# Fewer input products per pair of heads and more for the last pair, in a two-layer hybrid backbone on one core

## The chip, the cores and the metric

The kernel runs on one core of a Trainium2 chip. The metric is the device time of one execution in microseconds; the median of several executions is compared.

## The reference

A trunk of 256 context tokens and 512 latent tokens, 1024 channels wide, passes through two layers. The last layer needs outputs for the 512 latent tokens alone.

```python
def token_mixer(hc, hl, cos, sin, w_in, rw, cv, at, w_branch, w_out, ctx_out):
    zc = hc @ w_in
    zl = hl @ w_in
    rwc, cvc, atc, gtc = jnp.split(zc, IN_SPLIT_POINTS, axis=-1)
    rwl, cvl, atl, gtl = jnp.split(zl, IN_SPLIT_POINTS, axis=-1)
    o_rw_c, o_rw_l = rwkv_branch(rwc, rwl, *rw, ctx_out)
    o_at_c, o_at_l = attention_branch(atc, atl, *at, cos, sin, ctx_out)
    o_cv_l = conv_branch(cvl, *cv)
    out_l = merge_branches(o_rw_l, o_cv_l, o_at_l, gtl, w_branch, w_out)
    ...
```

The input projection w_in feeds three branches: RWKV-7 time mixing (16 heads of 64, a delta rule scanned forward and backward), a convolution of width 31, and grouped-query attention with rotary positions. Each branch is projected, gated by a sigmoid of further columns of the input projection, and summed; an output projection and a squared-ReLU MLP follow.

## The kernel before

The mixer of each layer runs in two stages: `rwkv_phase`, in which the time mixing is computed for eight pairs of heads, one after the other, and `merge_phase`, which holds attention, the convolution's norm and the projections.

**Jobs and units.** The input projection is cut into jobs of 128 output columns (`in_job`, `job`). A job has eight k steps, called units here. `fill(n)` issues n units: each has three products (high weights by high input, high by low, low by high), over 768 tokens as two matmuls of 384 columns each in layer 0, and over 512 tokens as one matmul of 512 columns each in most jobs of layer 1 (k, v and the rows 8 to 11 below run over 768 there too). Every fourth unit takes a new half of the weights, which `weight_half` loads on SyncE's queue and splits with one ScalarE and one VectorE operation.

**Spills.** 36 of the jobs produce columns that are needed only later: 8 tiles of queries (rows 0 to 7), 4 of keys and values (rows 8 to 11) and 24 of gates (rows 12 to 35). `spill` computes one and stores it to the scratch tensor z in HBM, from which `merge_phase` loads it again. The list `todo` gives their order: rows 0 to 19, 28 to 35, 20 to 27.

**A pair.** Iteration p of the loop in `rwkv_phase` queues the jobs of pair p+1 (k, r, v, some spills, two of the convolution), fills the first eight or so units, and then weaves generators: for pair p the merge (`rw_merge`, L928), the batch (`rw_batch`) and the chain over 12 chunks (`rw_chain`, L987 to L1006), the readout of pair p-1 (`rw_readout`), and for pair p+1 the preparation (`prep`), which ends in the solve (`rw_solve`), a serial run of VectorE operations between two kinds of transposes (L886 at its start, L895 and L896 at its end). The next iteration's merge needs the solve's result. `rw_kk` begins the preparation with the squares of k (L721). Each `yield` of a generator names some microseconds, and `pe` turns them into units at the rate that `weave` is given: the queued units by `span` for pairs 0 to 6, the setting `last` for the last one. The iteration of the last pair queues no pair but all spills that are left, and adds `att_stats`.

**How many spills each iteration gets.** `early` spills go into the opening. `todo_c(p)` spreads 32 - `rest` of them over the iterations 0 to 6. The others wait for the last pair. With `rest` at 9 these are 3, 4, 3, 3, 3, 4, 3 in both layers, and then 9 in layer 0 and 8 in layer 1.

**The load stage of attention.** `att_prep` loads keys, values and queries from z, turns the keys (`rope`, L522) and transposes the values (L590), and issues what is left of the jobs in parts: a third of them behind each of the two keys, half of the rest behind each of the two values. `merge_phase` issues the last of them, closes the pool of the input's halves hh and hl, and opens in its place the pool of the operand's halves oh and ol for the first projection.

The text above is program order. When the kernel is built, a scheduler orders each engine's instructions by this order and by what its own model holds ready, so a unit may run ahead of an instruction that waits. `behind` ties the merge's first matmuls to stand after the last unit issued ahead of the weave.

Of the kernel before, what the change touches and what calls it, by code (L numbers as in the profile page):

```python
# [44 lines left out]

SCHED = [dict(open=1.3, early=4, tap0=1, tap2=0, step=1.0, merge=1.2, sums=0, rest=9, ln=9, pad=1, last=1.15, span=78),
         dict(open=1.2, early=5, tap0=0.8, tap2=0, step=1.0, merge=1.4, sums=0, rest=9, ln=9, pad=1, last=0.85, span=76)]


def shape_constants():
# [24 lines left out]
class Kern:  # L77
# [1088 lines left out]
    def rwkv_phase(s, l, P, T):  # L1166
# [3 lines left out]
        with ExitStack() as rc:  # L1170
# [22 lines left out]
            lat = T != TOK  # L1193
            F = s.sched = SCHED[l]
            s.tdebt, s.tratio = 0.0, F['tap0']
# [298 lines left out]
```

## Time and profile before

| | us |
|---|---|
| median of 3 runs | 4302.82 |
| lowest and highest run | 4300.85, 4306.18 |
| profiled execution | 4305.05 |
| its span, first to last instruction | 4303.3 |
| mean granted clock over the span | 0.969 |

The profile comes from one execution; the predicted changes are made against its time. TensorE is the busiest engine. A busy engine in the profile has an instruction under way; matmuls overlap, so the same busy time can hold few or many of them, and the count beside it tells which. The granted clock is given as a share of 2.4 GHz, and 0.50 is its lower level.

In layer 0 the merges of the eight pairs begin at 223.0, 355.5, 496.5, 632.5, 773.5, 913.0, 1054.5 and 1195.0 us, and in layer 1 at 2592.0, 2707.5, 2833.5, 2961.0, 3081.0, 3199.0, 3322.5 and 3440.5 us (to half a microsecond). The stretches in the rows below run from one to the next; the last pairs end at about 1310 and 3519.5 us, where the load stage begins.

### The profile page before, as it was taken

To read this page: it belongs to the slowest core of one execution; us is meant where nothing else is said; L and a number is where in the kernel's file an instruction comes from. 1 tells how busy PE (TensorE), PEld (TensorE's weight loads), DVE (VectorE), ACT (ScalarE), POOL (GpSimd) and SP (SyncE) were. 2 spreads that over 40 slices of the span, in tenths; PEclk is the share of its full clock that TensorE was granted. 3 is DMA by queue.
4 is the path that set the end of the run, shared out by engine and by line. 5 is a ranking of instruction groups with operands and counts; after the bars stand their busy time and mean duration, and the time that the engine had idled before them with its cause. 6 is when DMAs were issued, how large, how long until landed. Compare 5 with 4: busy or idle time off the path is not lost.

```text
span 4303.3 us, 76623 instructions
## 1 busy us (share of the span) xinstructions
PE 4083.1 (95%) x31232; PEld 3360.6 (78%) x31232; DVE 2712.4 (63%) x5126; ACT 1829.2 (43%) x3426; POOL 254.8 (6%) x221
## 2 busy tenths in 40 slices
PE   6999999999998989899999899999999989898998
PEld 4988888888886679689999677877777765575886
DVE  3788888898855554332233478788889855554344
ACT  3444444444434442332222355455555534433332
POOL 0000000000001022100000200000000000121001
PEclk8999999999999999999999899999999979998998
DMA  4212221112134234343332131112122232242332
GB/s 167 80 49 63 59 62 57 49 55 71 58 102 165 70 116 154 126 147 118 101 98 62 64 90 54 55 59 59 59 65 61 84 125 76 68 138 61 96 96 79
DMA packets 443591, 367.70 MB, mean 85 GB/s; under 512 B 19662, under 2 KB 391528, under 8 KB 437096
## 3 DMA queue, kind: packets, MB, share of 16 engines
q1 hardware_dynamic: 422504, 283.10, 21.9%
q10 hardware_dynamic: 20736, 79.70, 5.1%
q8 instruction: 247, 4.05, 0.4%
q14 instruction: 104, 0.85, 0.1%
HBM read 301.38 MB, written 53.48 MB: 82 GB/s over the span
## 4 chain that ended last, share of the span: by engine, by line
PE 78%; DVE 11%; ACT 4%; issue 3%; DMA 2%; POOL 2%; SPq 0%; ACTq 0%; DVEq 0%; POOLq 0%
PE mm L412 29%; PE mm L389 21%; PE g L828 3%; PE g L634 2%; PE g L955 2%; PE g L966 2%; PE sp L987 2%; PE sp L991 2%; PE S L613 1%; PE g L875 1%; PE g L1071 1%; PE yp L1006 1%; DVE wl L332 1%; DVE A L892 1%; DVE Z L891 1%
## 5 line engine op out<-in xcount | busy, mean ns | idle before, releaser
L328 ACT ACTIVATE wh<-raw 128x512 fp32r<-128x512 f32 x700 | 441.4, 631 | 1218.4 <-PE mm L389 562.9
L332 DVE TENSOR_TENSOR wl<-raw,wh 128x512 fp32r<-128x512 f32 x700 | 500.6, 717 | 692.8 <-ACT wh L328 678.6
L412 PE MATMUL mm<-hh,wh 128*128 128x384 f32 (+1 forms) x2072 | 658.9, 378 | 10.0 <-ACT hh L347 4.0
L412 PE MATMUL mm<-hl,wh 128*128 128x384 f32 (+1 forms) x2072 | 626.0, 362 | 7.2 <-POOL hl L330 7.2
L412 PE MATMUL mm<-hh,wl 128*128 128x384 f32 (+1 forms) x2072 | 619.1, 361 | 2.5 <-DVE wl L332 2.4
L472 DVE SCALAR_TENSOR_TENSOR cv<-u,dw,cv 128x783 f32<-128x783 f32 (+1 forms) x480 | 426.7, 889 | 1.5
L412 PEld LDWEIGHTS mm<-hh,wh 128*128 128x128 f32 x2072 | 367.8, 191 | 61.8 <-issue 9.8
L412 PEld LDWEIGHTS mm<-hl,wh 128*128 128x128 f32 x2072 | 383.9, 191 | 34.4 <-POOL hl L330 10.0
L412 PEld LDWEIGHTS mm<-hh,wl 128*128 128x128 f32 x2072 | 384.0, 192 | 29.8 <-DVE wl L332 4.5
L412 PE MATMUL mm<-oh,wh 128*128 128x384 f32 (+1 forms) x768 | 252.3, 383 | 10.4 <-DVE acc L1320 6.0
L412 PE MATMUL mm<-ol,wh 128*128 128x384 f32 (+1 forms) x768 | 240.0, 365 | 10.6 <-POOL ol L330 10.6
L389 PE MATMUL mm<-hh,wh 128*128 128x384 f32 (+1 forms) x768 | 239.1, 366 | 6.3 <-ACT hh L347 3.6
L389 PE MATMUL mm<-hl,wh 128*128 128x384 f32 (+1 forms) x768 | 238.2, 365 | 5.5 <-POOL hl L330 5.0
L412 PE MATMUL mm<-oh,wl 128*128 128x384 f32 (+1 forms) x768 | 239.4, 365 | 0.0
L389 PE MATMUL mm<-hh,wl 128*128 128x384 f32 (+1 forms) x768 | 235.8, 362 | 0.0
L389 PE MATMUL mm<-fh,wh 128*128 128x384 f32 (+1 forms) x768 | 230.0, 353 | 0.0
L389 PE MATMUL mm<-fh,wl 128*128 128x384 f32 (+1 forms) x768 | 229.9, 353 | 0.0
L389 PE MATMUL mm<-fl,wh 128*128 128x384 f32 (+1 forms) x768 | 229.5, 352 | 0.0
L412 PEld LDWEIGHTS mm<-oh,wh 128*128 128x128 f32 x768 | 139.9, 190 | 51.5 <-ACT wh L328 13.6
L993 ACT ACTIVATE S<-sp,lam 128x64 f32<-128x64 f32 x352 | 94.4, 310 | 192.1 <-PE sp L991 172.4
L389 PEld LDWEIGHTS mm<-hh,wh 128*128 128x128 f32 x768 | 142.2, 192 | 37.7 <-ACT wh L328 15.9
L892 DVE TENSOR_TENSOR A<-A,Z 128x30 f32<-128x30 f32 (+14 forms) x480 | 159.0, 331 | 12.2
(300 smaller groups left out, 7078.5 us busy)
## 6 DMA issues: line engine op xcount, KB each, us to landing
raw<-in_w_in_dram SPq DMA_DIRECT2D x316, 256.0 KB
raw<-in_w_ff_dram SPq DMA_DIRECT2D x256, 256.0 KB
wmod<-in_w_mod_dram ACTq DMA_DIRECT2D x48, 1024.0 KB
raw<-in_w_branch_dram SPq DMA_DIRECT2D x96, 256.0 KB
z<-f ACTq DMA_DIRECT2D x40, 384.0 KB
gt<-z SPq DMA_DIRECT2D x24, 384.0 KB
raw<-in_w_out_dram SPq DMA_DIRECT2D x32, 256.0 KB
z<-f ACTq DMA_DIRECT2D x32, 256.0 KB
```

The costliest lines, as they stand in the source:

```text
L328: s.last_hi = nc.scalar.activation(out=hi, in_=src, func=AF.Copy)
L332: nc.vector.tensor_tensor(out=lo, in0=src, in1=hi.bitcast(F32), op=ALU.subtract)
L389: nc.tensor.matmul(ps[:, b, :t1 - t0], lhsT=w[:, k % 4, :], rhs=a[:, t0:t1], start=k == 0 and f == 0, stop=k == KT - 1 and f == 2)
L412: s.last_mm = nc.tensor.matmul(s.jps[:, b, :t1 - t0], lhsT=w[:, k % 4, :], rhs=a[:, t0:t1], start=k == 0 and f == 0, stop=k == KT - 1 and ...
L472: s.tap_pin(nc.vector.scalar_tensor_tensor(out=hold['c'], in0=u[:, k:k + L], scalar=w(k), in1=hold['c'], op0=ALU.mult, op1=ALU.add))
L634: nc.tensor.matmul(op[:, :nq], lhsT=V[:, kk, kv * 128:kv * 128 + 128], rhs=PT[:, kk, :nq], start=kk == 0, stop=kk == nk // 128 - 1)
L828: nc.tensor.matmul(gp[h][:, q, 0:n, :], lhsT=BK[ROWS[h], 4 * g + q].rearrange("p a b -> p (a b)"), rhs=E[ROWS[h], 0:n, 4 * g + q, :], star ...
L892: nc.vector.tensor_tensor(out=X[:, k + 1:, 0:k], in0=X[:, k + 1:, 0:k], in1=tm, op=ALU.add)
L955: nc.tensor.matmul(wu[ROWS[h], q - q0], lhsT=TT[ROWS[h], q, :], rhs=KM[ROWS[h], q].rearrange("p a b -> p (a b)"), start=True, stop=True)
L966: nc.tensor.matmul(ap[ROWS[h], q - q0, 0:n, :], lhsT=W[ROWS[h], q, :], rhs=GB[ROWS[h], h, q, 0:n, :], start=True, stop=True)
L987: nc.tensor.matmul(sp[ROWS[h], d], lhsT=GB[d][:, h, q[d], 0, :], rhs=UV[d][:, h * 12 + q[d], :], start=d == 0, stop=d == 1 and k == 0)
L993: nc.scalar.activation(out=Sn[:, d], in_=sp[:, d], func=AF.Copy, scale=Q['lam', d][:, q[d]:q[d] + 1])
```

## The change

Three settings of the table `SCHED` change: `rest` from 9 to 11 in layer 0, and in layer 1 `rest` from 9 to 14 and `last` from 0.85 to 1.4.

```diff
-SCHED = [dict(open=1.3, early=4, tap0=1, tap2=0, step=1.0, merge=1.2, sums=0, rest=9, ln=9, pad=1, last=1.15, span=78),
-         dict(open=1.2, early=5, tap0=0.8, tap2=0, step=1.0, merge=1.4, sums=0, rest=9, ln=9, pad=1, last=0.85, span=76)]
+SCHED = [dict(open=1.3, early=4, tap0=1, tap2=0, step=1.0, merge=1.2, sums=0, rest=11, ln=9, pad=1, last=1.15, span=78),
+         dict(open=1.2, early=5, tap0=0.8, tap2=0, step=1.0, merge=1.4, sums=0, rest=14, ln=9, pad=1, last=1.4, span=76)]
```

The places that read them:

```python
            todo_c = lambda p: round((32 - F['rest']) * p / 7)
...
                    spills(todo_c(p + 1) - todo_c(p))
...
                else:
                    spills(len(todo))
...
                s.weave(len(s.jobs) / F['span'] if more else F['last'], *gs)
```

## Rows read from the trace of the kernel before

**Rows 1.** The page's first part: busy time, share of the span, instructions.
```profile
PE 4083.1 (95%) x31232; PEld 3360.6 (78%) x31232; DVE 2712.4 (63%) x5126; ACT 1829.2 (43%) x3426; POOL 254.8 (6%) x221
```

**Rows 2.** Layer 0, iterations 1, 2, 3, 6, last pair, load stage; busy by engine, clock.
```profile
core 0: us, PE busy (x) PEld busy (x) DVE busy (x) ACT busy (x) POOL busy (x), PEclk, DMA share, GB/s
355.50:496.50 141.00, 140.42 (x1469) 122.45 (x1469) 121.72 (x231) 68.98 (x138) 1.80 (x4) 1.00 0.21 62
496.50:632.50 136.00, 135.53 (x1423) 115.85 (x1422) 116.97 (x225) 66.83 (x135) 1.66 (x4) 1.00 0.20 60
632.50:773.50 141.00, 139.79 (x1423) 120.35 (x1421) 119.19 (x229) 67.28 (x136) 1.26 (x4) 0.96 0.18 56
...
1054.50:1195.00 140.50, 139.67 (x1446) 119.90 (x1444) 122.34 (x232) 68.27 (x137) 1.66 (x4) 1.00 0.20 61
1195.00:1310.00 115.00, 113.57 (x1230) 101.12 (x1231) 56.66 (x115) 44.82 (x98) 0.00 (x0) 1.00 0.34 106
1310.00:1360.00 50.00, 36.17 (x144) 23.59 (x143) 30.27 (x50) 23.07 (x45) 13.62 (x8) 0.90 0.68 238
```

**Rows 3.** Starts of iterations 2 and 3: squares of k, then TensorE's clock in iteration 3.
```profile
501.32 0.94 ACT L721 ACTIVATE A<-E,V 128x768 f32<-128x768 f32 x1 [0.24 <-DVE E L656]
638.82 0.94 ACT L721 ACTIVATE A<-E,V 128x768 f32<-128x768 f32 x1 [1.85 <-DVE E L656]
...
644.00:648.00 4.00, 4.00 (x69) 0.50 0.22 66
```

**Rows 4.** Around layer 1's last merge: solve's ends, a spill's copy, the merge (timeline).
```profile
3403.74 1.99 DVE L886 STREAM_TRANSPOSE A<-Z 128x1024 f32<-128x1024 f32 x1
...
3422.78 0.58 ACT L1112 ACTIVATE f<-mm 128x512 f32<-128x512 f32 x1
...
3438.69 1.96 DVE L895 STREAM_TRANSPOSE Z<-A 128x1024 f32<-128x1024 f32 x1
...
3440.79 0.95 PE L928 MATMUL g<-Z,GL 32*32 32x32 f32 x48 [1.60 <-DVE Z L895]
```

**Rows 5.** Fill matmuls (tile mm) in layer 1's iterations 4, 5, 6 before the solve.
```profile
3081.00:3162.00 81.00, 28.16 (x91) 0.96 0.19 60
...
3199.00:3283.00 84.00, 37.85 (x122) 0.96 0.21 65
...
3322.50:3403.00 80.50, 30.84 (x107) 1.00 0.21 63
```

**Rows 6.** Layer 1, iterations 1, 2, 3, 5, 6, last pair, load stage, ten cold microseconds.
```profile
2707.50:2833.50 126.00, 124.34 (x1290) 103.71 (x1290) 99.54 (x207) 63.82 (x129) 1.02 (x4) 0.95 0.21 61
2833.50:2961.00 127.50, 125.52 (x1291) 100.88 (x1291) 113.41 (x234) 68.61 (x138) 1.58 (x4) 1.00 0.21 61
2961.00:3081.00 120.00, 115.14 (x1219) 90.92 (x1219) 102.98 (x218) 64.13 (x131) 1.15 (x4) 0.99 0.20 59
...
3199.00:3322.50 123.50, 121.82 (x1246) 96.28 (x1246) 106.38 (x223) 65.27 (x134) 1.08 (x4) 0.97 0.20 61
3322.50:3440.50 118.00, 114.66 (x1200) 87.39 (x1200) 99.02 (x211) 64.41 (x134) 0.99 (x4) 1.00 0.25 77
3440.50:3519.50 79.00, 77.25 (x849) 63.20 (x850) 39.03 (x100) 28.90 (x73) 0.00 (x0) 0.74 0.24 73
3519.50:3572.00 52.50, 38.96 (x139) 22.67 (x139) 29.12 (x47) 22.34 (x44) 12.24 (x9) 0.93 0.58 192
...
3480.00:3490.00 10.00, 10.00 (x71) 9.15 (x72) 1.59 (x12) 1.03 (x4) 0.00 (x0) 0.50 0.01 2
```

**Rows 7.** First rope matmul of each load stage, with TensorE's idle time before it.
```profile
1318.99 2.04 PE L522 MATMUL g<-kraw,rope 128*128 128x512 f32 x2 [5.64 <-DMA qs<-z]
...
3530.12 1.19 PE L522 MATMUL g<-kraw,rope 128*128 128x512 f32 x1 [6.88 <-DVE kT L582]
```

**Rows 8.** Dense runs of matmuls, of 384 columns and of 512 (chain in time).
```profile
1661.90 8.54 PE mm L412 x48
...
3375.24 6.05 PE mm L412 x25
```

## The prediction

> **What bounds the kernel now.** I read the page's first part, then busy time and granted clock by stretches of one pair of heads, then the order of instructions around the ends of pairs, then the load stage of attention. TensorE is busy 95% of the span [rows 1], but busy counts matmuls in flight, so what a removed job is worth must be read from the stage it leaves. The change moves jobs (one weight tile through eight k steps) between three places; each has its own limit.
>
> First, a pair of layer 0. Iterations 1 and 5 carry four spill jobs, the others three. The four-job iteration took 141.0 us; the three-job one behind it 136.0; a three-job one behind a three-job one 141.0 again [rows 2]. (Not shown: iterations 4 and 5 took 139.5 and 141.5.) So a job of 8.54 us of dense matmuls [rows 8] costs 5 us or nothing. The reason is seen at the starts [rows 3]: behind the four-job pair the squares of k (L721) waited 0.24 us for VectorE, behind the three-job pair 1.85 us; in the second case VectorE was still in the solve's last transposes when the merge began, TensorE ran dry, and the clock stood at 0.50, its lower level, 1.2 of 2.4 GHz. With less fill the solve on VectorE ends last, not the matmuls.
>
> Second, a pair of layer 1. It has two parts. The solve on VectorE runs from 3403.74 to the transpose at 3438.69 [rows 4], some 37 us, and TensorE fills it with whatever jobs are free. The part before it took 81.0 us with 91 recorded fill matmuls, 80.5 with 107 and 84.0 with 122 [rows 5]: above about 107 a job costs, below it time is flat, and the clock is 0.96 at 91 against 1.00 at 107. Thinning further buys little.
>
> Third, the last pair of layer 1. Its merge waited 1.60 us for the solve, and spill jobs of the last pair ended before it, the one at 3422.78 among them [rows 4]; I count five of eight there (3417 to 3440). Program order does not hold the jobs: whatever is free is put into the wait. So only three jobs were left for what follows, and the last pair ran at a mean clock of 0.74, with a stretch of 10.00 us busy out of 10 at 0.50 [rows 6], where layer 0's last pair, full of jobs, held 1.00 [rows 2].
>
> Behind both last pairs lies the load stage: the first rope matmul waits 5.64 us in layer 0 and 6.88 us in layer 1 for its tiles [rows 7], with the mean clock at 0.90 and 0.93 [rows 2, 6].
>
> **The change part by part.** No instruction is added or removed; only places change. From todo_c, spill jobs per iteration go in layer 0 from 3,4,3,3,3,4,3 and 9 to 3 each and 11; in layer 1 from 3,4,3,3,3,4,3 and 8 to 3,2,3,2,3,2,3 and 13. The last weave has 57.1 us of yields in layer 0, thus 65 units (a unit is one k step) before and after; what is left for the load stage goes from 7 to 23. In layer 1 it has 55.5: 47 units at 0.85, 77 at 1.4, and 17 and 27 left. A unit is 8.54/8 = 1.07 us in layer 0 and 3 x 6.05/25 = 0.73 us in layer 1 [rows 8].
>
> (a) Pairs of layer 0. Iteration 1 becomes a three-job pair behind an undisturbed one: 141.0 to 136.0, -5. Iteration 2 now stands behind a three-job pair and gets the late squares and the cold start: 136.0 to 140, +4. Iterations 3 and 4: 0. Iteration 5: 141.5 to 140, -1.5. Iteration 6, 140.5 now [rows 2], also loses its undisturbed start: +4. Sum +1.5. If no start were cold, all would be 136 and the sum -19; if the starts cost 5 and nothing is saved, +10. I take the middle rows, since both kinds of start stand in this trace.
>
> (b) Load stage of layer 0: 16 units more, 17.1 us. The wait of 5.64 us takes a first part; the 50 us at 0.90 give back up to 5.0 us if the work there is dense. 17.1 - 5.6 - 5.0 = +6.5. Bounds: 17.1 if all of it stands behind the waits, about 0 if it also fills the small waits for POOL's halves of the operand. Queued behind the extra units is the release of hh and hl, and so the operand splits; these also wait for loads of their own, issued behind the z loads, so I take no extra delay; the upper bound has room for it. The weight loads of the moved jobs (two per job, on SP's queue) may now stand ahead of the z loads, and their stores stay on ACT's queue; issues alone don't bound either queue, so I put them at nothing, and their cost, if that is wrong, is a longer wait for the rope [rows 7].
>
> (c) Pairs of layer 1, from the lengths of the iterations [rows 6]. Iteration 1 loses two jobs (those of k and v, which run over all 768 tokens): 126.0 to an ordinary 118.5, -7.5. Iteration 2 takes over these two and drops two of 512: 127.5 to a four-job length, 123.5, -4. Iteration 3 loses one: -1. Iteration 5 goes from four to two: 123.5 to 118.5, -5. Iterations 4 and 6: 0. Against this I set +3 for thinner pairs at a lower clock, since the clock already falls at 91 fill matmuls [rows 5]. Sum -14.5. Bounds: 0, if the lost clock eats it; -28, if all 29.0 us (5 jobs) came back as they do from 122 to 107 fill matmuls (3.6 us of matmuls, 3.5 us of time).
>
> (d) Last pair and load stage of layer 1: 40 units, +29.0 us of dense work. The last pair's 79.0 us at 0.74 lose 20.5 us to the clock; with 37 units instead of 7 behind the merge it is as full as layer 0's, and I take all of it back. The 10 extra units left over last 7.3 us and fit the 6.88 us wait. The 52.5 us at 0.93 give 3.7. 29.0 - 20.5 - 6.9 - 3.7 = -2.1. Bounds: +22 (no clock back) and -6.
>
> Sum: +1.5 + 6.5 - 14.5 - 2.1 = -8.6 us. The profiled execution took 4305.05 us, its span 4303.3; 4305.05 - 8.6 = 4296.5. The median of the runs shown is 2.2 us lower, so the forecast is 4302.8 - 8.6 = 4294.2 us.
>
> A rule to weigh at (d): the lower clock stands beside a TensorE that is busy throughout [rows 6], so here many small matmuls, without idle time, go with it. The Trainium skill (TensorE: Matmul & The Clock Gate, Part 1: The HAM clock gate) ties the lower level to TensorE standing idle and the upper to its being busy. By that rule alone the last pair would not be cold for want of fill, and fill would not warm it; its result is the third rival.
>
> **The rivals.** *Pairs follow TensorE's work.* If the step from 141.0 to 136.0 for one job (8.54 us) holds everywhere, each us removed gives 0.6: layer 0 -10, layer 1 -17.4, with (b) and (d) as above: -23, 4280 us. For it: TensorE's 95%. Against it: the flat 81.0 and 80.5 [rows 5].
>
> *Thinned pairs go cold.* Iterations 3 to 6 of layer 1 each lose about 3 us more to the clock, as the cold start [rows 3] costs 4 to 5: (c) is -2.5 and the sum +3.4, 4306 us. For it: the clock at 91 fill matmuls. Against it: 107 to 91 cost only 0.5 us.
>
> *The clock does not come back.* The last pair of layer 1 stays at 0.74 with more fill, so 29.0 us are paid with only the wait of 6.88 us as cover: (d) is +22, the sum +15.6, 4318 us, slower. It decides by degrees: below two thirds of the 24.2 us the gain is gone, and below 0.3 the kernel is slower by more than 8.6 us. Against it: 1.00 in layer 0's last pair [rows 2].
>
> *The load stage does not cover.* The built order may put the rope matmuls before the extra units; TensorE then waits as now with the units behind: (b) 17.1, (d) +8.5, sum +12.6, 4315 us, slower. Against it: in both layers the fill now stands ahead of that wait.
>
> That the jobs do not land where the settings say is true already (five of eight ran ahead of the merge) and only shifts part of (c) into (d); it stays inside the range.
>
> **How the numbers follow.** Forecast 0.58, TensorE's work 0.15, cold pairs 0.12, no clock 0.08, no cover 0.07. A measurement of this kernel can tell about 0.2%, 8.6 us, from no change; the forecast lies on that line, so half of its chance goes to each side. Faster: 0.29 + 0.15 = 0.44. Same: 0.29 + 0.12 = 0.41. Slower: 0.15. Eight times in ten: from 4280, where the first rival ends, to 4309, which takes in the cold pairs and leaves out the two slower ones; the bounds of (a) to (d) do not all fall together.
>
> **What the profile after would show.** (a) iterations 1 to 6 of layer 0 all near 140 us, cold starts at 2 and 6 too. (b), (d) the wait before the first rope matmul gone or below 2 us, and the load stage of layer 0 longer by 4 to 9 us. (c) iterations 1 and 5 of layer 1 near 118.5, iteration 2 near 123.5. (d) the last pair of layer 1 near 80 us with a clock above 0.95. What would make it wrong: a built order that differs in many places, so that pairs that I take over unchanged move too, or a clock that falls in the thinned pairs of layer 1 below 0.93.

## Result and profile after

The changed kernel took 4359.6 us (median of 4 runs, 4356.56 to 4365.12) beside 4304.5 us for the kernel before (median of 4 runs, the three of the first table and one more): ratio 1.0129, interval 1.0112 to 1.0147. It is 55 us slower; 4294.2 us was forecast, with a range that ended at 4309. Its profiled span is 4363.3 us at a mean clock of 0.961 (before 4303.3 and 0.969).

The page's first part shows the same instructions and more time on TensorE [rows 1]: the work did not grow, it took longer.

```profile
PE 4130.5 (95%) x31232; PEld 3397.3 (78%) x31232; DVE 2708.2 (62%) x5126; ACT 1831.3 (42%) x3426; POOL 253.5 (6%) x221
```

Busy time and clock by stretches say where: in layer 0 iterations 1 to 3 and the load stage, then in layer 1 iterations 1 to 6, the last pair, the load stage, and 20 us of the last pair (busy by engine with counts, clock, DMA share, GB/s).

```profile
354.00:489.50 135.50, 135.25 (x1422) 115.65 (x1421) 117.16 (x225) 66.84 (x135) 1.65 (x4) 1.00 0.20 60
489.50:630.50 141.00, 139.78 (x1423) 120.59 (x1421) 119.14 (x228) 67.33 (x136) 1.25 (x4) 0.96 0.18 56
630.50:771.50 141.00, 139.74 (x1421) 120.10 (x1420) 119.56 (x229) 66.83 (x136) 1.74 (x4) 0.96 0.18 54
1300.00:1360.00 60.00, 52.87 (x262) 44.39 (x260) 32.16 (x53) 27.33 (x50) 15.27 (x8) 0.94 0.68 235
2711.00:2840.00 129.00, 126.33 (x1295) 105.18 (x1295) 109.00 (x226) 65.43 (x131) 1.28 (x4) 0.96 0.18 54
2840.00:2967.00 127.00, 123.79 (x1263) 99.41 (x1263) 101.49 (x216) 65.71 (x133) 1.02 (x4) 0.97 0.21 61
2967.00:3095.50 128.50, 117.12 (x1193) 91.15 (x1193) 108.42 (x227) 62.42 (x128) 0.63 (x4) 0.94 0.17 49
3095.50:3221.00 125.50, 118.15 (x1211) 92.21 (x1211) 95.22 (x204) 63.96 (x130) 0.64 (x4) 0.96 0.18 55
3221.00:3355.50 134.50, 121.94 (x1192) 95.19 (x1192) 108.93 (x228) 62.36 (x128) 1.26 (x4) 0.89 0.16 46
3355.50:3489.00 133.50, 125.53 (x1207) 95.47 (x1207) 98.46 (x209) 65.01 (x133) 0.64 (x4) 0.92 0.23 68
3489.00:3574.00 85.00, 84.19 (x875) 69.00 (x875) 31.67 (x90) 31.01 (x75) 0.00 (x0) 0.74 0.26 79
3574.00:3630.00 56.00, 48.76 (x189) 32.17 (x190) 30.18 (x46) 24.22 (x48) 11.48 (x8) 0.97 0.67 213
3530.00:3550.00 20.00, 20.00 (x111) 17.11 (x112) 3.38 (x19) 2.78 (x8) 0.00 (x0) 0.50 0.10 27
```

Against [rows 6], iterations 3, 5 and 6 of layer 1 are longer by 8.5, 11.0 and 15.5 us, with fewer matmuls in two of them and 7 more in the last. TensorE's idle time grew in them: 12.6 us in iteration 5, where before had 1.7. So something other than TensorE ends last there. It is the solve. VectorE's timeline of iteration 5 of after: start, four operations in the middle, end.

```profile
3311.23 1.97 DVE L886 STREAM_TRANSPOSE A<-Z 128x1024 f32<-128x1024 f32 x1 [1.39 <-ACT Z L863]
...
3322.97 0.74 DVE L472 SCALAR_TENSOR_TENSOR cv<-u,dw,cv 128x512 f32<-128x512 f32 x1
3323.63 0.40 DVE L891 TENSOR_TENSOR Z<-A 128x234 f32<-128x234 f32 x1
3323.94 0.74 DVE L472 SCALAR_TENSOR_TENSOR cv<-u,dw,cv 128x512 f32<-128x512 f32 x1
3324.61 0.40 DVE L892 TENSOR_TENSOR A<-A,Z 128x234 f32<-128x234 f32 x1
...
3353.61 1.99 DVE L895 STREAM_TRANSPOSE Z<-A 128x1024 f32<-128x1024 f32 x1
```

L891 and L892 are the solve's serial steps. Between two of them stands a tap of the convolution (L472), one of the 31 products that it sums up for each tile: 0.66 us from its start to the next step's. From L886 to L895 this solve took 42.4 us; that of iteration 6 took 43.9, where before has 3403.74 to 3438.69, 35.0 us [rows 4]. The taps in the solves of iterations 5 and 6 of after, and in that of iteration 6 of before (VectorE's busy time on line 472 and its count, clock, DMA share, GB/s):

```profile
3311.00:3353.40 42.40, 14.08 (x19) 0.95 0.19 54
3443.40:3489.00 45.60, 14.19 (x19) 1.00 0.37 107
```

```profile
3403.70:3440.60 36.90, 5.26 (x7) 1.00 0.37 110
```

TensorE's timeline shows who waits: TensorE sat idle for 2.50 us before the last merge (1.60 before [rows 4]). The rope matmuls of the two load stages, by contrast, lost their waits [rows 7].

```profile
3489.46 1.49 PE L928 MATMUL g<-Z,GL 32*32 32x32 f32 x48 [2.50 <-DVE Z L895]
...
1312.85 1.96 PE L522 MATMUL g<-kraw,rope 128*128 128x512 f32 x4 [1.57 <-DMA rope<-in_rope_dram]
...
3588.28 1.96 PE L522 MATMUL g<-kraw,rope 128*128 128x512 f32 x4 [0.84 <-DMA qs<-z]
```

### The profile page after: what moved, and what is told of

Read it like the earlier page. It is cut to its first block, busy times and chain, and to the rows that moved or that the text cites. A ratio compares the mean times of both kernels' runs of the same rounds, so it can differ in the third digit from the quotient of the medians.

```text
span 4363.3 us, 76605 instructions
## 1 busy us (share of the span) xinstructions
PE 4130.5 (95%) x31232; PEld 3397.3 (78%) x31232; DVE 2708.2 (62%) x5126; ACT 1831.3 (42%) x3426; POOL 253.5 (6%) x221
## 5 line engine op out<-in xcount | busy, mean ns | idle before, releaser
L332 DVE TENSOR_TENSOR wl<-raw,wh 128x512 fp32r<-128x512 f32 x700 | 501.4, 717 | 700.4 <-ACT wh L328 686.8
L412 PE MATMUL mm<-hh,wl 128*128 128x384 f32 (+1 forms) x2072 | 634.8, 367 | 15.6 <-DVE wl L332 15.5
L412 PEld LDWEIGHTS mm<-hh,wh 128*128 128x128 f32 x2072 | 373.4, 194 | 66.8 <-issue 9.0
L472 DVE SCALAR_TENSOR_TENSOR cv<-u,dw,cv 128x783 f32<-128x783 f32 (+1 forms) x480 | 424.7, 885 | 0.9
L389 PE MATMUL mm<-hh,wl 128*128 128x384 f32 (+1 forms) x768 | 234.5, 360 | 0.0
L828 PEld LDWEIGHTS g<-E,BK 64*128 64x128 f32 x1536 | 141.1, 197 | 40.7 <-issue 22.6
L828 PE MATMUL g<-E,BK 64*128 64x128 f32 (+1 forms) x1536 | 163.3, 294 | 8.3 <-ACT key L912 2.7
```

What stands on the lines that cost most here:

```text
L332: nc.vector.tensor_tensor(out=lo, in0=src, in1=hi.bitcast(F32), op=ALU.subtract)
L389: nc.tensor.matmul(ps[:, b, :t1 - t0], lhsT=w[:, k % 4, :], rhs=a[:, t0:t1], start=k == 0 and f == 0, stop=k == KT - 1 and f == 2)
L412: s.last_mm = nc.tensor.matmul(s.jps[:, b, :t1 - t0], lhsT=w[:, k % 4, :], rhs=a[:, t0:t1], start=k == 0 and f == 0, stop=k == KT - 1 and ...
L472: s.tap_pin(nc.vector.scalar_tensor_tensor(out=hold['c'], in0=u[:, k:k + L], scalar=w(k), in1=hold['c'], op0=ALU.mult, op1=ALU.add))
L828: nc.tensor.matmul(gp[h][:, q, 0:n, :], lhsT=BK[ROWS[h], 4 * g + q].rearrange("p a b -> p (a b)"), rhs=E[ROWS[h], 0:n, 4 * g + q, :], star ...
```

## Experiments

Two theories. A: with fewer spill jobs per pair, the jobs of the next pair come earlier and reach into the wait for the solve. A tap is kept behind the VectorE operation ahead of it in program order (`tap_pin`), often one of those jobs; so it comes to stand between the solve's steps, and the pair ends later. B: the thinned fill itself is to blame, because TensorE goes cold (its clock falls to the lower level) or idle.

The table holds all kernels: layer 0's pairs 0 to 6; from layer 0's last merge to layer 1's first; layer 1's pairs 0 to 6; in these the sum of the seven solves (L886 to L895) and the taps in them; from layer 1's last merge to the end. All in us, from one profiled execution each (merge starts to half a microsecond). One execution can lie well off its kernel's median: that of e1_l0 by 14.4 us, those of e3_last, e7_bhold_last and e14_rest7 by about 7. Three kernels, before, e1_l0 and e15_l0_rest7, hold the same instructions in layer 1, in the same order on VectorE and ScalarE, and their pairs differ by up to 5 us, their ends by 5.5; smaller differences between two rows say nothing.

| kernel | ratio, interval | L0 pairs | between | L1 pairs | solves | taps | end |
|---|---|---|---|---|---|---|---|
| before | | 972 | 1397 | 848.5 | 241.9 | 41 | 862.8 |
| after | 1.0129, 1.0112 to 1.0147 | 965.5 | 1408.5 | 894 | 275.6 | 84 | 874.3 |
| e1_l0 | 1.0023, 1.0010 to 1.0036 | 968.5 | 1407.5 | 853.5 | 242.1 | 41 | 864.0 |
| e2_rest | 1.0145, 1.0122 to 1.0169 | 964.5 | 1392 | 892 | 266.9 | 72 | 882.2 |
| e3_last | 1.0035, 1.0020 to 1.0050 | 976.5 | 1395.5 | 858 | 253.0 | 53 | 865.6 |
| e4_hold | 1.0031, 1.0018 to 1.0044 | 961 | 1397 | 863.5 | 218.7 | 0 | 872.1 |
| e5_bhold | 0.9991, 0.9975 to 1.0007 | 964.5 | 1389 | 857.5 | 216.4 | 0 | 858.0 |
| e7_bhold_last | 1.0000, 0.9988 to 1.0012 | 967 | 1387 | 859 | 216.4 | 0 | 869.3 |
| e10_rest12 | 1.0052, 1.0033 to 1.0071 | 964 | 1398 | 858.5 | 254.6 | 59 | 876.4 |
| e11_rest_hold | 1.0042, 1.0028 to 1.0057 | 971.5 | 1387 | 859.5 | 217.9 | 0 | 882.3 |
| e12_hold_tap06 | 1.0015, 1.0001 to 1.0029 | 973.5 | 1386.5 | 866 | 214.8 | 1 | 862.0 |
| e13_rest7_hold | 1.0011, 1.0000 to 1.0021 | 976.5 | 1389.5 | 862 | 220.0 | 0 | 860.2 |
| e14_rest7 | 1.0013, 1.0004 to 1.0021 | 964.5 | 1396 | 848 | 238.5 | 27 | 866.9 |
| e15_l0_rest7 | 1.0036, 1.0022 to 1.0050 | 974.5 | 1406 | 852 | 242.1 | 41 | 858.5 |

**One part alone.** The three settings apart: e1_l0 has only layer 0's, e2_rest only layer 1's `rest`, e3_last only layer 1's `last`.

```diff
 e1_l0:   layer 0  rest=9   ->  rest=11
 e2_rest: layer 1  rest=9   ->  rest=14
 e3_last: layer 1  last=0.85 -> last=1.4
```

> Only the layer 0 half of the change: rest is 11 there, layer 1 stays as before. By the two traces layer 0 gives +3 us (its pairs 6 to 8 us shorter, its load stage 11 longer). Both theories say the same here: 3 to 6 us slower than before, 4308 to 4311 us, within what can be told from no change. If it takes more than 15 us, the loss is not in layer 1 and both theories fall.

> Only rest = 14 in layer 1; last stays at 0.85 and layer 0 as before. Theory A, taps in the solve: in iterations 1 to 5 as many convolution taps stand between the solve's transposes as in the changed kernel (12, 6, 18, 6, 19 in the built order, against 0, 8, 9, 4, 9 before), in iteration 6 only 7 instead of 19. Iterations 1 to 5 take about 30 us longer than before, iteration 6 about 7 (its part ahead of the solve), in all some 35 to 45 us slower than before: 4340 to 4350. Theory B, thinned pairs go cold and the fill is missing: the same 45 us over iterations 1 to 6, iteration 6 not shorter than in the changed kernel (133 us), and more on top from a last pair that is thinner still: 4355 or more.

> Only last = 1.4 in layer 1; both rest settings stay at 9, so no pair loses a job. Theory A: 19 instead of 7 taps stand in the solve of iteration 6, which gets about 8 us longer (126 instead of 118); the last pair gains at most that back: 3 to 10 us slower than before. Theory B: no pair is thinned, the last pair is denser and warmer: 0 to 8 us faster than before, iteration 6 at 118.

Layer 1's `rest` alone gives as large a loss as the whole change (the three parts don't add up): its pairs take 892 us, after's 894. In time all three missed theory A's figures, upwards: e1_l0 is some 10 us slower where both theories had 3 to 6, e3_last some 15 for 3 to 10, and e2_rest took 4354.8 us, above A's 4350 and at the edge of B's 4355. But iteration 6 of e2_rest took 125 us, as A had it, not B's 133; what A left out is the end, 19 us longer than before. e3_last is the cleanest single case: no job changes its pair, yet iteration 6 is longer, 128.5 us for 118 [rows 6], at a clock of 1.00 in both, so not by a cold TensorE. VectorE's timeline and TensorE's merge behind it:

```profile
3405.53 2.00 DVE L886 STREAM_TRANSPOSE A<-Z 128x1024 f32<-128x1024 f32 x1
...
3451.34 1.92 DVE L895 STREAM_TRANSPOSE Z<-A 128x1024 f32<-128x1024 f32 x1
...
3453.41 0.95 PE L928 MATMUL g<-Z,GL 32*32 32x32 f32 x48 [3.38 <-DVE Z L895]
```

The solve starts 80.8 us after the merge, as before (81.0), and then takes 45.8 instead of 35.0 us, with 19 taps in it for 7. Twelve taps, three weight splits and some 2 us more of waits in the chain make the 10.8 us.

**The taps held.** In layer 1 every tap is queued on VectorE behind the end of the solve that stands ahead of it in program order; nothing else in the program is changed. e4_hold does it to after, e5_bhold to before, e7_bhold_last to before with `last` at 1.4, e11_rest_hold to before with `rest` at 14.

```diff
     def tap_pin(s, ins):
         s.tc.keep_in_program_order(ins)
+        if s.solved is not None and s.sched is SCHED[1]:
+            s.behind(ins, s.solved)
...
-        nc.vector.transpose(out=s.Z[:, 768:1792].rearrange("p (u t) -> p t u", t=32), in_=X)
+        s.solved = nc.vector.transpose(out=s.Z[:, 768:1792].rearrange("p (u t) -> p t u", t=32), in_=X)
...
             s.tdebt, s.tratio = 0.0, F['tap0']
+            s.solved = None
```

> The changed kernel with one thing undone: in layer 1 every convolution tap is queued on VectorE behind the end of the solve that stands before it in program order, so none stands inside a solve (80 did). No other instruction is added or left out. Theory A: the solves of iterations 1 to 6 fall from 37 to 44 us to 29 to 34; the taps are then paid beside other work: 30 to 50 us faster than the changed kernel, 4310 to 4330. Theory B: the solves are not what lost the time; the part ahead of the solve stays at 85 to 90 us or grows by the taps that now stand there: 4345 or more.

> The kernel before with the taps of layer 1 queued behind the solve, as in e4_hold, and no job moved. 37 taps leave the solves of iterations 1 to 6. Theory A (taps in the solve, at 0.66 us each): these solves fall from 29 to 37 us to 28 to 32, some 20 us in all; part of it is paid back ahead of the solve, as in e4_hold, where 80 taps cost some 27 us there: 5 to 15 us faster than before. Theory B (thin fill, cold clock) adds: this kernel differs from e4_hold in layer 1 by five jobs more in the pairs, so its parts ahead of the solve show a clock of 0.96 or more and 80 to 88 us, against 87 to 100 us at 0.85 to 0.96 there. If the parts ahead of the solve are as long as in e4_hold, thin fill is not what made them long.

> e5_bhold with last = 1.4 in layer 1. In e3_last the same setting put 12 more taps into the last solve and cost 10 us there. With the taps queued behind the solve, theory A expects no such loss: iteration 6 as in e5_bhold within 3 us, the whole within 5 us of e5_bhold. If last = 1.4 costs 10 us here too, it was not by the taps.

> Kernel before with layer 1's rest at 14 alone (five jobs fewer in its pairs, last pair's density .85, layer 0 as before), and in layer 1 every conv tap queued on VectorE behind the end of the pair's solve. With rest 14 and free taps the seven pairs took 892 us where before has 848.5; with rest 9 and held taps 857.5. Theory A (the lengthening is taps that come into the solve's chain): held, the five jobs fewer cost little, pairs 857 to 868 us, each solve 29 to 33 us instead of 37 to 44, the stretch behind the last merge 872 to 882 us, whole time 15 to 30 us over the kernel before (ratio 1.0035 to 1.007). Theory B (the thinned fill itself makes TensorE's part longer): the parts ahead of the solve lengthen, pairs above 885 us, whole time 40 to 60 us over the kernel before (ratio 1.009 to 1.014) although no tap lies in a solve.

The start of iteration 6's solve in e11_rest_hold: the steps (here L893, L894) follow one another with no tap between.

```profile
3410.46 1.99 DVE L888 STREAM_TRANSPOSE A<-Z 128x1024 f32<-128x1024 f32 x1 [0.53 <-ACT Z L865]
...
3413.49 0.25 DVE L893 TENSOR_TENSOR Z<-A 128x84 f32<-128x84 f32 x1
3413.77 0.24 DVE L894 TENSOR_TENSOR A<-A,Z 128x84 f32<-128x84 f32 x1
```

The four corners stand in the table. `rest` from 9 to 14 costs layer 1's pairs 43.5 us with free taps (848.5 to 892) and 2 us with held ones (857.5 to 859.5); `last` at 1.4 costs 9.5 us free and 1.5 held. Of the 43.5 us, 25.0 stand in the solves (241.9 to 266.9), and held they shrink to 1.5 (216.4 to 217.9): for this part theory A is shown (how the taps get into the solve is read from the program and was not tested by itself). The other 18 us stand ahead of the solves of iterations 1 to 6 (512.5 us in before, 530.7 in e2_rest). Held, this part doesn't grow either (546.4 and 547.2), but there it already carries the held taps, 34 us more than in before, and these may hide what a thinner fill costs. So whether the 18 us come from taps or from fill is not shown. In e10_rest12, three jobs fewer, this part did not grow (510.4), and the pairs' 10 us are the solves'.

The numbers set for theory A were met by e4_hold, e7_bhold_last and, but for tenths of a microsecond, e11_rest_hold (solves 28.4 to 32.5 us, end 882.3). e5_bhold missed: 5 to 15 us less than before was expected, and 0.9991 is not clear of no change. Its solves are 25.5 us shorter, but its taps are paid ahead of them, and more dearly: the pairs take 9 us more. As its parts ahead are nearly as long as e4_hold's (550.1), thin fill did not make those long. And the held kernels tell one thing more: the five jobs fewer bring nothing back. The parts of iterations 1 to 6 ahead of the solve, as windows; the lines of iterations 3 and 4 and the sum of the six, first e5_bhold, then e11_rest_hold:

```profile
2941.50:3036.30 94.80, 89.42 (x966) 67.86 (x967) 72.84 (x140) 48.59 (x102) 0.77 (x4) 0.93 0.17 52
3070.00:3161.30 91.30, 85.89 (x956) 64.63 (x957) 72.27 (x139) 48.83 (x102) 1.27 (x4) 0.94 0.17 51
...
sum 547.90, PE 528.47 PEld 411.21 DVE 442.89 ACT 294.59 POOL 6.97; mean PE 88.08 PEld 68.53 DVE 73.82 ACT 49.10 POOL 1.16
```

```profile
2938.50:3034.80 96.30, 91.46 (x950) 70.56 (x950) 72.04 (x139) 47.87 (x100) 1.21 (x4) 0.86 0.14 43
3067.50:3165.00 97.50, 92.39 (x960) 70.48 (x960) 73.58 (x141) 47.26 (x100) 1.21 (x4) 0.88 0.16 51
...
sum 548.30, PE 527.89 PEld 413.42 DVE 435.13 ACT 282.19 POOL 7.68; mean PE 87.98 PEld 68.90 DVE 72.52 ACT 47.03 POOL 1.28
```

Sum and busy time are equal to about half a microsecond, though by the prediction's estimate 29 us of dense matmuls were taken out of these pairs. The clock is lower: length times the share missing from 1.00 gives 20 us lost in e5_bhold's six parts and 45 in e11_rest_hold's. That difference is about what was taken out. That the clock is the cause is argued from this, not shown; theory B keeps this part.

**Sizes between and beyond.** e10_rest12 stops at three jobs fewer. e14_rest7 turns the change round, two jobs more in layer 1's pairs; e13_rest7_hold does so with held taps; e15_l0_rest7 does it in layer 0; e12_hold_tap06 holds the taps and lowers the share of them at a pair's opening.

```diff
 e10_rest12:     layer 1  rest=9 -> rest=12
 e14_rest7:      layer 1  rest=9 -> rest=7
 e13_rest7_hold: layer 1  rest=9 -> rest=7, taps held as above
 e15_l0_rest7:   layer 0  rest=9 -> rest=7
 e12_hold_tap06: layer 1  tap0=0.8 -> tap0=0.6, taps held as above
```

> Layer 1 rest = 12, three jobs fewer in the pairs instead of five, nothing else. In the built order 55 taps stand in the solves of iterations 1 to 6, against 37 before and 68 in e2_rest. Theory A: 18 x 0.66 = 12 us in the solves; with some 5 from the part ahead of them 12 to 22 us slower than before. Theory B alone (each job taken out costs about the same, 57/5 us as in e2_rest): 34 us slower.

> Kernel before with layer 1's rest at 7 alone (two jobs more in its pairs), taps free. In the built order the taps inside the seven solves of layer 1 are 27 instead of 41. Theory A (each tap in the solve costs 0.66 to 0.9 us of the pair): the solves become 9 to 13 us shorter in sum, pairs 838 to 848 us, the stretch behind the last merge 848 to 856, whole time 8 to 20 us below the kernel before (ratio 0.995 to 0.998). Theory B (a fuller pair follows TensorE's work, 7.3 to 8.5 us more for two jobs): pairs 855 to 858, ratio 0.999 to 1.001.

> The change turned round: kernel before with two jobs more in layer 1's pairs instead of five fewer (rest 7, last pair's density .85), and every conv tap of layer 1 queued behind the end of the solve. With held taps, rest 9 gave 857.5 us for the seven pairs and 858 behind the last merge; rest 14 gave 859.5 and 882.3. If a job in the pairs is hidden by the wait for the solve (0.4 us each between rest 14 and 9), pairs 857 to 861 and the stretch behind the last merge 845 to 852 (4.9 us a job): whole time 6 to 12 us below the kernel before (ratio 0.997 to 0.9985). If a job added to a pair already full costs its own time (3.5 us of every 3.6), pairs 863 to 868, and the ratio is 0.999 to 1.001.

> Kernel before with layer 0's rest at 7 alone: two jobs more in its pairs, two fewer behind them. With rest at 11 the stretch from layer 0's last merge to layer 1's first grew by some 11 us and the seven pairs became 3 to 11 us shorter. If both go linearly, that stretch becomes 8 to 12 us shorter and the pairs 5 to 9 us longer: ratio 0.998 to 1.0005. If the load stage has nothing to give back below rest 9 (its first rope matmul already waits 5.64 us), the stretch stays within 3 us and the ratio is 1.001 to 1.002.

> Kernel before with the taps of layer 1 queued behind the end of each solve, and layer 1's share of taps at a pair's opening at 0.6. Nothing is moved between stages. With held taps alone the part ahead of the solve took 85 to 96 us and the solve 29.5 to 32 us. Theory A (what the solve gained is given back by taps that all come at once ahead of it): with the taps spread otherwise the parts ahead become 3 to 5 us shorter each, whole time 5 to 15 us below the kernel before (ratio 0.9965 to 0.999). Theory B (the parts ahead are set by the fill and the clock, not by taps): parts ahead as with held taps alone, 85 to 96 us, ratio 0.998 to 1.001.

None is clearly faster than the kernel before. e10_rest12 lies between: solves 12.7 us longer, pairs 10, end 13.6; in time, some 22 us slower, it is at the upper end of A's 12 to 22 and below B's 34. e14_rest7 met neither expectation: 14 taps fewer stand in the solves, but these are only 3.4 us shorter in sum, and the pairs stay at 848. In its iteration 2 a weight split that stands in the chain waits itself, and the chain with it (VectorE's timeline):

```profile
2912.45 1.97 DVE L886 STREAM_TRANSPOSE A<-Z 128x1024 f32<-128x1024 f32 x1 [1.39 <-ACT Z L863]
...
2926.05 0.69 DVE L332 TENSOR_TENSOR wl<-raw,wh 128x512 fp32r<-128x512 f32 x1 [3.23 <-ACT wh L328]
...
2948.77 2.00 DVE L895 STREAM_TRANSPOSE Z<-A 128x1024 f32<-128x1024 f32 x1
```

With three taps fewer than before, this solve took 36.3 us for 35.4: the 3.23 us of waiting for ScalarE's half of the split ate what the taps gave. So what counts is every VectorE operation that lands in the chain, with its own wait. Over the 91 solves of layer 1 in all kernels but e15_l0_rest7 a straight fit gives 0.54 us for a tap, 0.42 for a shift operation of k, r or v (L656), 0.79 for a weight split (L332) and 23.8 us for the bare chain, with 0.6 us (one standard deviation) unexplained. That is an estimate, and it holds such waits only on average. By it the 43 taps more in after's solves make some 23 of their 33.6 us, and 22 more shift operations, which came in with them, 9.

e13_rest7_hold missed as well: its pairs, 862 us, came near the dearer expectation, but the end became no shorter, 860.2 for 858.0. e12_hold_tap06 missed its gain too. Against e5_bhold it moved single parts ahead of the solve, iteration 3's from 94.6 to 85.7 us, those of iterations 1, 2 and 5 up by 3 to 6; their sum did not fall (551.2 for 546.4; pairs 866). So the spread of the taps moves these parts about, but this setting saves nothing. e15_l0_rest7 missed both ends: with fewer jobs behind layer 0's pairs the stretch between the layers grew by 9 us. Its load stage ran dry, in busy time and clock:

```profile
1310.00:1365.00 55.00, 32.62 (x121) 20.98 (x122) 31.73 (x57) 22.38 (x48) 12.41 (x6) 0.76 0.59 210
```

The clock there is 0.76 where before has 0.90 [rows 2].

## Why the prediction was wrong

**(c), the step that failed.** Forecast -14.5 us, bounds -28 to 0; measured +45.5 (848.5 to 894). Two assumptions were in it. First, the solve was taken as given, "some 37 us", filled by TensorE with whatever is free. It is a chain on VectorE, and VectorE's order is rebuilt with the jobs: the seven solves grew by 33.6 us in sum. The sign was at hand: in before, L886 to L895 already varied from 29.4 us (iteration 1, no tap) to 36.9 (iterations 3 and 5, nine taps each). Only the last solve was read. Second, the five jobs taken out were credited with 17.5 us, and below about 107 fill matmuls the part ahead of the solve was read as flat. These parts grew by 12 us instead: down by 4.9 and 3.5 in iterations 1 and 2, up by 20 in 3 to 6. In iterations 5 and 6 of after they are longer with fewer fill matmuls and at a lower clock than in [rows 5] (fill matmuls on TensorE, clock, DMA share, GB/s):

```profile
3221.00:3311.00 90.00, 30.63 (x95) 0.87 0.13 41
3355.50:3443.00 87.50, 28.36 (x84) 0.88 0.15 47
```

Iterations 4 and 6, set at 0 because their number of jobs stays, took 7.5 and 15.5 us more. The closing sentence named this ("pairs that I take over unchanged move too"), and the clock below 0.93 with it: iterations 5 and 6 had 0.89 and 0.92. The fallen clock had a rival and a price, the moved pairs had neither.

**(d).** Forecast -2.1, bounds -6 to +22; measured +11.5 (862.8 to 874.3), of which the last pair has 6.0 (85.0 for 79.0) and the load stage 3.5. The clock stayed at 0.74, as in the rival "The clock does not come back". Much of the fill did not come where it was expected. ScalarE's copies of spills next to the merge at 3489.46 are

```profile
3488.02 0.58 ACT L1112 ACTIVATE f<-mm 128x512 f32<-128x512 f32 x1
3533.48 0.60 ACT L1112 ACTIVATE f<-mm 128x512 f32<-128x512 f32 x1 [0.36 <-PE mm L412]
```

Six of the thirteen jobs ran ahead of the merge in the longer solve, and then none ended for 45 us. The last pair holds 91 recorded fill matmuls (tile mm) for 57 in before, but only 18 of them in its first 41 us:

```profile
3489.00:3530.00 41.00, 9.23 (x18) 4.67 (x18) 0.00 (x0) 0.00 (x0) 0.75 0.32 99
3530.00:3574.00 44.00, 24.59 (x73) 15.40 (x73) 0.00 (x0) 2.16 (x4) 0.73 0.21 61
```

In e4_hold, the same settings with held taps, the last pair has 125 fill matmuls and a clock of 0.94:

```profile
3442.50:3522.00 79.50, 78.68 (x914) 63.08 (x915) 47.13 (x113) 34.33 (x80) 0.00 (x0) 0.94 0.33 98
```

That could be the amount as well as the place. For the place speaks e13_rest7_hold: in the first 79 us behind the merge it has 71 fill matmuls and after 75, at 0.93 and 0.72; 30 to 60 us behind the merge stand 36 of them in the one and 17 in the other. So that fill can warm this stage was right; that the added units would lie close behind the merge was not, although the prediction had read that five of eight already ran ahead of it. And even warm the end took 872.1 us in e4_hold, 14.1 more than in e5_bhold: about half of the 29.0 us moved is hidden there. The setting `last` has a price of its own: with 1.4 alone and no job moved, the end of e7_bhold_last is 11.3 us longer than e5_bhold's.

**(a).** Forecast +1.5; the pairs of layer 0 took 965.5 us for 972. The three kernels with two jobs fewer there, after among them, span 961 to 968.5, those with before's layer 0 span 964 to 976.5: a gain of a few us at most, within the bounds. (The bound of -19 is a slip: its rows give -23.5.) Iterations 1 to 6 took 135.5, 141.0, 141.0, 136, 136 and 143 us. The sum had set 136, 140, 141, 139.5, 140 and 144.5, so the first three and the last came about as set, the cold starts at 2 and 6 among them (0.96 each), and 4 and 5 did not. Such lengths are in part chance: iteration 3, from whose 141.0 us in before it was read what a job costs, took 136.3 in e2_rest and e5_bhold, which hold the same order in layer 0. So what came as set is no proof of the reading.

**(b).** Forecast +6.5, bounds 0 to 17.1. Between the layers after and e1_l0 take 1408 us, kernels with before's layer 0 and free taps 1392 to 1398: about +12; with held taps 1397 for 1386.5 to 1389.5, +9. The mechanism held (wait of 5.64 us down to 1.57, TensorE busy 52.87 of 60 us at 0.94), the size was 9 to 12 us instead of 6.5.

**The rivals.** "Pairs follow TensorE's work" is out: e11_rest_hold has the work removed and no time saved. "Thinned pairs go cold" named a part of it: ahead of the solves of iterations 3 to 6, where it had set 12 us, 20 were lost. "The load stage does not cover" is out by the rope waits. None of them held the 33.6 us. The rule of the Trainium skill that was weighed at (d) (TensorE: Matmul & The Clock Gate, Part 1: The HAM clock gate) ties the lower level to an idle TensorE; the trace of after disagrees once more, with 20.00 of 20 us busy at 0.50 (3530 to 3550), and e4_hold's warmer last pair speaks against it too.

What stays open is what sets the part of a pair ahead of the solve: neither fewer jobs (e11_rest_hold) nor the other spread of taps (e12_hold_tap06) shortened its sum over the iterations, and no run sets the clock apart from the fill.

## What to carry over

Where a serial chain on one engine ends a stage, list what else stands on that engine's queue inside it, for every iteration, before pricing work on another engine. Moving matmuls between stages rebuilds that queue: count the operations that come with a job or are pinned behind it, and price the chain by them. And a job put "behind" a point in program order may run ahead of it if the scheduler finds a wait there, so fill meant to warm a stage has to be held there; no run here did that directly.

## What was not expected of the hardware

The solve's length repeats with the order: iteration 1 took 29.45, 29.44 and 29.44 us in before, e1_l0 and e3_last, which are separate executions, and 37.36 and 37.37 in after and e2_rest. The pairs of layer 0 do not: after and e4_hold hold the same program there, yet iteration 3 took 141.0 us in one and 136.7 in the other, and iteration 5 136.3 and 140.7. Whether a start is cold moves from run to run by about 4.5 us a pair, so a single pair's length is no evidence for a change of that size.
